# The last layer norm of a hybrid decoder layer: statistics on 128x3 values, spread by identity products, and five tiles scaled on GpSimd

## The chip, the cores and the metric

The kernel runs on one core of a Trainium2 chip. The metric is the device time of one execution in microseconds, the median of several runs. Times inside the execution count from the start of the profiler's span. The engines are TensorE (PE; its weight loads are PEld), VectorE (DVE), ScalarE (ACT), GpSimd (POOL) and SyncE (SP), which issues most of the DMAs.

## What is computed

One inference step of a decoder layer for 256 prompt tokens and 8 x 8 new tokens, 320 tokens together, D = 2048 channels. Two token mixers (an mLSTM and an HGRN2 recurrence) read one input projection; the merged branches go through an output projection, a layer norm, a feed-forward block and a second layer norm. Beside y the new recurrent states are outputs, Cp and Sp (prompt) and Cs and Ss (samples) among them.

```python
x1 = layernorm(alpha * x + merged @ w_out, ln1_g, ln1_b)
hid = square(relu(x1 @ w_up))
y = layernorm(alpha * x1 + hid @ w_down, ln2_g, ln2_b)
# layernorm over the 2048 channels of each token:
mu = mean(x); var = mean(square(x - mu))
(x - mu) * rsqrt(var + 1e-5) * g + b
```

The change concerns the second of these layer norms.

## The kernel before, in words

Activations are held with channels on partitions: 16 tiles of 128 channels x 320 tokens (`self.acc`, one buffer f3m). So the mean and the variance of a token are sums over partitions and over the 16 tiles. Weights stream through in 128x128 blocks. Each fp32 weight and activation is split into a high and a low part in fp32r, and a product is three fp32r matmuls (`mm`, recorded at L341); the statistics use plain fp32 matmuls, which the profile shows as two instructions each. ACT's instructions are recorded at L335, SP's DMAs at L344.

The order of the work on each engine is written by a small scheduler in the kernel (`Sched`). Work is described by generator chains that ask for an engine with an estimated cost, wait for events (`wait`, `post`), and acquire and release buffers (`acq`, `rel`). The scheduler keeps an estimated clock for each engine, and places an instruction when the estimate says that its inputs are ready. Each engine then executes its instructions in exactly that order, waiting where an input is late. The main loop `run_main` lays down the weight matmuls and lets the chains put theirs between them (`pump`). The estimates decide the order alone; the times come from the chip.

In the last weight stage (w_down, f = 3) each finished tile is added on DVE (`ev_dn`, L2138) and enters two running sums over the tiles: S1 of the values and S2 of their squares (`ln_sum`, L1986 and L1987, squares on ACT). A rough mean per token was subtracted before (L2137), so that the sums are well conditioned.

- `ln_pre`: as soon as tile 14 is in, S1 and S2 are multiplied by a 128x128 matrix of ones on TensorE, 320 tokens wide. That sums over the partitions and leaves each sum on all 128 partitions of a PSUM bank. These two products lie between the last weight matmuls.
- `ln_final`: tile 15 (z) and its square are added to the same banks by two further ones products. Then, on values of 128x320: the mean and its square on ACT; variance (L2020) and eps (L2023) on DVE; Ln and Exp on ACT; one Newton step of three DVE instructions (L2027 to L2029). The event "end" says that 1/sigma is ready.
- `y`: DVE subtracts the mean and multiplies by 1/sigma in steps of two tiles, 128x640 (L2154). `yb_`: ACT multiplies by g and adds b, tile by tile; SP issues the y DMA of two tiles.

Meanwhile TensorE makes the prompt states: `m_C`, 8 products of six fp32r matmuls of 512 columns (Cp), each copied from PSUM by ACT and sent out, and `h_S`, 8 products of 256 columns (Sp), copied in four pairs by ACT or DVE. The DMAs of y, Cp and Sp all stand in SP's queue, in the scheduler's order. POOL's queue holds memsets and, late, the six loads for `m_C` (L1193, L1194), the last of them at 2228 us.

Of the kernel before, what the change touches and what calls it, by code (L numbers as in the profile page):

```python
# [246 lines left out]
def post(ev):  # L247
    return ("set", ev)
# [48 lines left out]
class Program:  # L297
# [883 lines left out]
    def m_C(self, h):  # L1181

        late = h >= 2
        if late:

            yield wait(self.rest_ev)
            x = self.wr.rearrange("p u n -> p (u n)")[:, 1536 * (h - 2):1536 * (h - 1)]
            xk, xv = x[:, 0:512].rearrange("p (s k) -> p s k", s=2), x[:, 512:1536]
        else:
            k = yield acq(self.kx)  # L1190
            w = yield acq(self.vx)
            xk, xv = k[:, 1].bitcast(F32), w[:, 1024:2048].bitcast(F32)
        yield ("pool", 1000, lambda: self.nc.gpsimd.dma_start(xk, self.kD[h].rearrange("(s p) k -> p s k", p=128)))  # L1193
        t = yield ("pool", 1000, lambda: self.nc.gpsimd.dma_start(  # L1194
            xv.rearrange("p (n k) -> p n k", k=128), self.vtD[h].rearrange("j (i p) k -> p (j i) k", p=128)))
        e = Ev()
        e.t = t + 5000.0
        yield wait(e)
        if late:
            k = yield acq(self.kx)  # L1200
            w = yield acq(self.vx)
        yield from self.split(xk, k[:, 0], k[:, 1], 512)
        yield from self.split(xv, w[:, 0:1024], w[:, 1024:2048], 1024)
        yield wait(self.main_end)
        for c in range(2):
            if h or c:
                yield wait(self.ln[1]["fin"])
            b = yield acq(self.mbank)
            yield ("pe", 6 * pe_r(512), lambda: [self.mm(
                b.rearrange("p (j v) -> p j v", j=4), k[:, x, s, 128 * c:128 * c + 128], self.of_tokens(w[:, 1024 * y:1024 * y + 1024], s), start=n == 0, stop=n == 5)  # L1210
                for n, (s, x, y) in enumerate((s, x, y) for s in range(2) for x, y in ((0, 0), (0, 1), (1, 0)))])
# [728 lines left out]
    def ln_add(self, n, j, z, pre):  # L1940
# [49 lines left out]
    def ln_pre(self, n):  # L1990

        p = self.ln[n]["p"] = yield acq(self.sbank, 2)
        for i in range(2):
            yield ("pe", pe_f(TOK), lambda: self.mm(p[i][:, :TOK], self.ones, self.lnb[i], start=True, stop=False))
        yield post(self.ln[n]["pre"])

    def ln_final(self, n, z):

        v = self.nc.vector
        st = self.ln[n]  # L2000
        M, RS, X, T = (self.lnb[i] for i in (3, 4, 5, 6))
        q = yield acq(self.tmp)
        t = yield ("act", act(TOK), lambda: self.A(q, z, AF.Square))
        if n:
            yield wait(st["pre"])
        else:
            S1, S2 = self.lnb[0], self.lnb[1]
            yield ("dve", dve(TOK), lambda: v.tensor_tensor(S1, S1, z, ALU.add), (t - act(TOK) - LAT,))
            yield ("dve", dve(TOK), lambda: v.tensor_tensor(q, S2, q, ALU.add), (t,))
            st["p"] = yield acq(self.sbank, 2)  # L2010
            yield wait(self.slack(1000.0))
        p1, p2 = (p[:, :TOK] for p in st["p"])
        yield ("pe", pe_f(TOK), lambda: self.mm(p1, self.ones, z if n else S1, start=n == 0, stop=True))
        yield ("pe", pe_f(TOK), lambda: self.mm(p2, self.ones, q, start=n == 0, stop=True))
        yield rel(self.tmp, q)
        yield post(st["fin"])
        t = yield ("act", act(TOK, True), lambda: self.A(M, p1, scale=1.0 / D))
        st["m"].t = t
        yield ("act", act(TOK, True), lambda: self.A(T, p1, AF.Square, scale=1.0 / D))
        yield ("dve", dve(TOK, True), lambda: v.scalar_tensor_tensor(X, p2, 1.0 / D, T, ALU.mult, ALU.subtract))  # L2020
        for p in st["p"]:
            yield rel(self.sbank, p)
        yield ("dve", dve(TOK, mode=2), lambda: v.tensor_scalar(T, X, 0.0, EPS, ALU.max, ALU.add))  # L2023
        yield post(st["x"])
        yield ("act", act(TOK), lambda: self.A(RS, T, AF.Ln))
        yield ("act", act(TOK), lambda: self.A(RS, RS, AF.Exp, scale=-0.5))
        yield ("dve", dve(TOK), lambda: v.scalar_tensor_tensor(X, T, -0.5, RS, ALU.mult, ALU.mult))  # L2027
        yield ("dve", dve(TOK), lambda: v.tensor_tensor(X, X, RS, ALU.mult))  # L2028
        yield ("dve", dve(TOK), lambda: v.scalar_tensor_tensor(RS, X, 1.5, RS, ALU.add, ALU.mult))  # L2029
        yield post(st["end"])  # L2030
        if n == 0:

            yield ("dve", dve(TOK), lambda: v.tensor_tensor(T, T, RS, ALU.mult))

    def ln_x(self):

# [110 lines left out]
    def y(self):  # L2147
# [1 line left out]
        v = self.nc.vector  # L2149
        st = self.ln[1]  # L2150

        def step(i, n, by, op):
            z = self.acc[:, i:i + n, :]
            return ("dve", dve(n * TOK), lambda: v.tensor_tensor(z, z, by.unsqueeze(1).to_broadcast([128, n, TOK]), op), (0.0,))  # L2154

        sub = lambda i, n=2: step(i, n, self.lnb[3], ALU.subtract)
        yield wait(st["m"])
        yield sub(0, 1)
        yield wait(st["x"])
        yield sub(1, 1)  # L2160
        yield sub(2)
        yield wait(st["end"])
        for i, n in (*((2 * i, 2) for i in range(7)), (14, 1), (15, 1)):
            t = yield step(i, n, self.lnb[4], ALU.mult)
            for j in range(i, i + n):
                self.s.spawn(self.yb_(j, self.acc[:, j, :]), 0, t)
            if i < 12:
                yield sub(i + 4)

    def yb_(self, j, z):  # L2170
        g, b = self.vec[:, V_G2 + j:V_G2 + j + 1], self.vec[:, V_B2 + j:V_B2 + j + 1]
        yield ("act", act(TOK, False, 2), lambda: self.A(z, z, AF.Identity, scale=g, bias=b))
        if j % 2 or j == 14:
            q = slice(j if j > 13 else j - 1, j + 1)
            yield ("sp", 620, lambda: self.dma(self.d["y"][:, q, :], self.acc[:, q, :]))


    def run(self, pool):
# [18 lines left out]
        self.ln = [dict(c=Ev(), x=Ev(), end=Ev(), pre=Ev(), m=Ev(), fin=Ev(), s=[Ev() for _ in range(KT)]) for _ in range(2)]  # L2197
# [85 lines left out]
```

## Time and profile before

| | |
|---|---|
| median of 3 runs | 2266.55 us (2266.45 to 2266.98) |
| profiled execution, time | 2266.39 us |
| profiled execution, span | 2264.5 us |
| TensorE busy | 2256.1 us, granted clock 0.999 |
| DVE busy | 1422.4 us |
| ACT busy | 1014.1 us |
| POOL busy | 13.4 us |
| last add of a w_down tile | 2239.09 us |
| last DMA issued, end of issue | 2259.81 us |

The profile is of one execution; its rows give start, duration, engine, line and the tiles written and read, with the number of instructions that a row merges. A duration of a matmul contains its way through the array, so that matmuls that follow each other overlap in the rows; the distance of their starts is what they take. "[1.44 <-PE ...]" is idle time ahead of an instruction, and what ended it.

### The profile page before, as it was taken

Reading aid. Unit: us, or ns where it says so; the run is one execution under the profiler, and the core shown is the slowest. Engines: PE = TensorE matmul, PEld = TensorE weight load, DVE = VectorE, ACT = ScalarE, POOL = GpSimd, SP = SyncE. Lnnn points to the kernel's source line nnn. Section 1 sums busy time; section 2 is a strip of 40 time slices with the busy share of each in tenths; the row PEclk is TensorE's granted clock in tenths of the full one; section 3 lists DMA queues with packets and bytes.
Section 4 is the critical chain, followed back from the end, with each engine's and each line's share of the span. In section 5 each row is a group of like instructions: output and inputs, shape, how many; then the busy total and the mean of one; then the engine's idle time right before and its main releaser. Section 6 shows DMA issues by size and latency. Waiting matters only on the chain.

```text
span 2264.5 us, 39898 instructions
## 1 busy us (share of the span) xinstructions
PE 2256.1 (100%) x15938; PEld 2217.7 (98%) x15938; DVE 1422.4 (63%) x2490; ACT 1014.1 (45%) x1586; POOL 13.4 (1%) x41
## 2 busy tenths in 40 slices
PE   9999999999999999999999999999999999999998
PEld 9999999999999999999999999999999999999998
DVE  6757667788888876555555769444444444444566
ACT  5444444455555565444434446333433343334434
POOL 0000000000000000000000000000000000000000
PEclk9999999999999999999999999999999999999999
DMA  7888797677677765555556544444444444444644
GB/s 240 305 270 287 224 289 245 200 232 235 197 228 217 235 193 173 173 173 173 174 175 208 193 147 153 151 151 151 149 149 149 149 149 151 150 151 152 198 149 159
DMA packets 251171, 432.94 MB, mean 191 GB/s; under 512 B 106844, under 2 KB 146916, under 8 KB 250984
## 3 DMA queue, kind: packets, MB, share of 16 engines
q1 hardware_dynamic: 250088, 427.24, 58.3%
q0 software_dynamic: 896, 3.15, 0.5%
q8 instruction: 125, 2.05, 0.4%
q14 instruction: 62, 0.51, 0.1%
HBM read 377.30 MB, written 53.00 MB: 190 GB/s over the span
## 4 chain that ended last, share of the span: by engine, by line
PE 99%; ACT 1%; DVE 0%; issue 0%; ACTq 0%; POOL 0%; POOLq 0%
PE bank L341 99%; ACT f3m L335 0%; ACT oC L335 0%; PE bank L1346 0%; PE bank L1118 0%; PE bank L1042 0%; ACT f2l L335 0%; ACT oS L335 0%; DVE f3m L2154 0%; PE bank L1678 0%; ACTq L2279 0%; DVE f2l L2029 0%; DVE f2l L2027 0%; DVE f2l L2028 0%; DVE f2l L2020 0%
## 5 line engine op out<-in xcount | busy, mean ns | idle before, releaser
L341 PE MATMUL bank<-xh,wh 128*128 128x320 f32 x2408 | 751.9, 313 | 0.0
L341 PE MATMUL bank<-xh,wl 128*128 128x320 f32 x2408 | 743.1, 310 | 0.0
L341 PE MATMUL bank<-xl,wh 128*128 128x320 f32 x2408 | 740.2, 308 | 0.0
L335 ACT ACTIVATE wh<-wr 128x1024 fp32r<-128x1024 f32 (+1 forms) x432 | 452.9, 1048 | 582.2 <-PE bank L341 551.8
L511 DVE TENSOR_TENSOR wl<-wr,wh 128x1024 fp32r<-128x1024 f32 x423 | 516.7, 1222 | 304.1 <-ACT wh L335 298.3
L341 PEld LDWEIGHTS bank<-xh,wh 128*128 128x128 f32 x2408 | 452.0, 188 | 6.9 <-issue 3.9
L341 PEld LDWEIGHTS bank<-xl,wh 128*128 128x128 f32 x2408 | 452.3, 188 | 2.7
L341 PEld LDWEIGHTS bank<-xh,wl 128*128 128x128 f32 x2408 | 453.0, 188 | 0.0
L335 ACT ACTIVATE bb<-wr 128x1024 fp32r<-128x1024 f32 x181 | 191.8, 1060 | 352.6 <-PE bank L341 339.9
L511 DVE TENSOR_TENSOR bb<-wr,bb 128x1024 fp32r<-128x1024 f32 x179 | 219.1, 1224 | 159.7 <-ACT bb L335 159.6
L341 PE MATMUL bank<-xh,bb 128*128 128x320 f32 (+1 forms) x1280 | 284.1, 309 | 0.0
L341 PE MATMUL bank<-ra,bb 128*128 128x320 f32 x1264 | 283.3, 308 | 0.0
L341 PE MATMUL bank<-rxb,bb 128*128 128x320 f32 x1112 | 255.0, 309 | 0.0
L341 PE MATMUL bank<-ra,wh 128*128 128x320 f32 x892 | 248.8, 308 | 0.0
L341 PEld LDWEIGHTS bank<-xh,bb 128*128 128x128 f32 x1280 | 214.6, 188 | 0.0
L341 PEld LDWEIGHTS bank<-ra,bb 128*128 128x128 f32 x1264 | 210.6, 188 | 0.2
L341 PE MATMUL bank<-xl,bb 128*128 128x320 f32 (+1 forms) x640 | 197.5, 309 | 0.0
L341 PEld LDWEIGHTS bank<-rxb,bb 128*128 128x128 f32 x1112 | 188.3, 188 | 0.2
L341 PE MATMUL bank<-rxb,wl 128*128 128x320 f32 x596 | 183.7, 308 | 0.0
L341 PE MATMUL bank<-rxb,wh 128*128 128x320 f32 x596 | 183.7, 308 | 0.0
L341 PEld LDWEIGHTS bank<-ra,wh 128*128 128x128 f32 x892 | 161.4, 188 | 0.0
L341 PEld LDWEIGHTS bank<-xl,bb 128*128 128x128 f32 x640 | 120.2, 188 | 0.0
(332 smaller groups left out, 2103.7 us busy)
## 6 DMA issues: line engine op xcount, KB each, us to landing
wr<-wt SPq DMA_DIRECT2D x602, 512.0 KB
rx<-C SPq DMA_DIRECT2D x34, 256.0 KB
Cs<-rx SPq DMA_DIRECT2D x34, 256.0 KB
f<-C SPq DMA_DIRECT2D x30, 256.0 KB
Cs<-f SPq DMA_DIRECT2D x30, 256.0 KB
f<-xT SPq DMA_DIRECT2D x26, 160.0 KB
f<-S SPq DMA_DIRECT2D x8, 512.0 KB
f3h<-S SPq DMA_DIRECT2D x8, 512.0 KB
```

Source lines behind the costliest of these rows:

```text
L335: return self.nc.scalar.activation(out, in_, func, **kw)
L341: self.nc.tensor.matmul(*a, **kw)
L511: self.V().tensor_tensor(lo, raw, hi.bitcast(F32), ALU.subtract)
```

## The change

- For the second layer norm `ln_pre` goes. `ln_final` adds tile 15 and its square to S1 and S2 on DVE, and `ln_rows` follows.
- `ln_rows`: 24 small products with 32 columns of S1 or S2 as the weights and a single column of ones as the moving operand leave the sums with tokens on partitions: 128 x 3 values for each of the sums (320 tokens in three blocks; the last two overlap). Square, variance, eps, Ln, Exp and Newton step work on 128x3. One ones product of S1 leaves the sum of the values on all partitions in a PSUM bank (`pm`), as before.
- 1/sigma comes back to the wide form by three products with the identity matrix as the moving operand and a column of 1/sigma, broadcast to 128 columns, as the weights (`spread`, into the bank `pr`).
- `y` reads both from PSUM: the subtraction is one scalar_tensor_tensor with the factor -1/D, the multiplication a tensor_tensor. Tile 0 stands alone at the beginning and tile 15 at the end; subtraction and multiplication of a pair follow each other.
- `yb_`: tiles 4, 6, 8, 10 and 12 are scaled by GpSimd in place of ACT; a y DMA waits for both of its tiles. In the built program a library reload stands in POOL's queue ahead of its first tile.
- `m_C`: three of the six matmuls of the second Cp product stand ahead of the spread and three behind it; ACT's Cp copies stand behind the Exp.

```diff
@@ m_C
             if h or c:
-                yield wait(self.ln[1]["fin"])
+                yield wait(self.ln[1]["end" if h else "fin"])
             b = yield acq(self.mbank)
-            yield ("pe", 6 * pe_r(512), lambda: [self.mm(...)
+            jobs = [(s, x, y) for s in range(2) for x, y in ((0, 0), (0, 1), (1, 0))]
+            cuts = (0, 6) if h else (0, 1, 2, 3, 6) if c else range(7)
+            for lo, hi in zip(cuts, cuts[1:]):
+                if h == 0 and c and lo == 3:
+                    yield post(self.ln[1]["c1"])
+                    yield wait(self.ln[1]["end"])
+                yield ("pe", (hi - lo) * pe_r(512), lambda: [self.mm(...)
+                    for n, (s, x, y) in enumerate(jobs) if lo <= n < hi])
+            yield wait(self.ln[1]["exp"])
@@ ln_add
-        if j == 14 and n:
-            self.s.spawn(self.ln_pre(n), 0)
@@ ln_final
+        S1, S2 = self.lnb[0], self.lnb[1]
+        t1 = yield ("dve", dve(TOK), lambda: v.tensor_tensor(S1, S1, z, ALU.add), (t - act(TOK) - LAT,))
+        t2 = yield ("dve", dve(TOK), lambda: v.tensor_tensor(q, S2, q, ALU.add), (t,))
         if n:
-            yield wait(st["pre"])
+            yield from self.ln_rows(st, S1, q, t1, t2)
+            return
@@ new
+    def ln_rows(self, st, S1, S2, t1, t2):
+        v = self.nc.vector
+        blocks = (0, 128, TOK - 128)
+        sm = yield acq(self.sm)
+        T, X, RS = (sm[:, 3 * i:3 * i + 3] for i in range(3))
+        p, pm, pr = yield acq(self.sbank, 3)
+        st["pm"], st["pr"] = pm[:, 0:TOK], pr[:, 0:TOK]
+        t = yield ("pe", 700.0, lambda: [self.mm(
+            p[32 * g:32 * g + 32, o:o + 1], S[:, b + 32 * g:b + 32 * g + 32], self.one, start=True, stop=True, skip_group_check=True)
+            for o, (S, b) in enumerate((S, b) for S in (S1, S2) for b in blocks) for g in range(4)], (t1, t2))
+        st["m"].t = (yield ("pe", pe_f(TOK), lambda: self.mm(st["pm"], self.ones, S1, start=True, stop=True))) + 2 * LAT
+        yield post(st["fin"])
+        yield ("act", 200.0, lambda: self.A(T, p[:, 0:3], AF.Square, scale=1.0 / D), (t + 2 * LAT,))
+        yield ("dve", 200.0, lambda: v.scalar_tensor_tensor(X, p[:, 3:6], 1.0 / D, T, ALU.mult, ALU.subtract))
+        yield ("dve", 200.0, lambda: v.tensor_scalar(T, X, 0.0, EPS, ALU.max, ALU.add))
+        yield post(st["x"])
+        yield ("act", 200.0, lambda: self.A(RS, T, AF.Ln))
+        yield ("act", 200.0, lambda: self.A(RS, RS, AF.Exp, scale=-0.5))
+        yield post(st["exp"])
+        t = yield ("dve", 600.0, lambda: (
+            v.scalar_tensor_tensor(X, T, -0.5, RS, ALU.mult, ALU.mult), v.tensor_tensor(X, X, RS, ALU.mult),
+            v.scalar_tensor_tensor(RS, X, 1.5, RS, ALU.add, ALU.mult)))
+        yield post(st["n"])
+        def spread():
+            for i, b in enumerate(blocks):
+                o = max(b, 128 * i)
+                n = min(128, TOK - o)
+                self.mm(pr[:, o:o + n], RS[:, i:i + 1].to_broadcast([128, 128]), self.ident[:, o - b:o - b + n], start=True, stop=True)
+        yield wait(st["c1"])
+        st["end"].t = (yield ("pe", 3 * 218.0, spread, (t,))) + 2 * LAT
@@ y
-        sub = lambda i, n=2: step(i, n, self.lnb[3], ALU.subtract)
+        def sub(i, n=2):
+            z = self.acc[:, i:i + n, :]
+            return ("dve", dve(n * TOK, True), lambda: v.scalar_tensor_tensor(z, wide(st["pm"], n), -1.0 / D, z, ALU.mult, ALU.add), (0.0,))
+        def mult(i, n=2):
+            z = self.acc[:, i:i + n, :]
+            return ("dve", dve(n * TOK, True), lambda: v.tensor_tensor(z, z, wide(st["pr"], n), ALU.mult), (0.0,))
...
+        yield wait(st["x"], st["m"])
         yield sub(0, 1)
-        yield wait(st["x"])
-        yield sub(1, 1)
-        yield sub(2)
+        yield wait(st["n"])
+        yield sub(1)
         yield wait(st["end"])
-        for i, n in (*((2 * i, 2) for i in range(7)), (14, 1), (15, 1)):
-            t = yield step(i, n, self.lnb[4], ALU.mult)
+        for i, n in ((0, 1), *((2 * i + 1, 2) for i in range(7)), (15, 1)):
+            if i > 1:
+                yield sub(i, n)
+            t = yield mult(i, n)
...
-            if i < 12:
-                yield sub(i + 4)
@@ yb_
-        yield ("act", act(TOK, False, 2), lambda: self.A(z, z, AF.Identity, scale=g, bias=b))
-        if j % 2 or j == 14:
-            q = slice(j if j > 13 else j - 1, j + 1)
+        if j in (4, 6, 8, 10, 12):
+            yield ("pool", 700.0, lambda: self.nc.gpsimd.tensor_scalar(z, z, g, b, ALU.mult, ALU.add))
+        else:
+            yield ("act", act(TOK, False, 2), lambda: self.A(z, z, AF.Identity, scale=g, bias=b))
+        yield post(self.y_ev[j])
+        if j % 2 == 0 or j == 15:
+            q = slice(j if j in (0, 15) else j - 1, j + 1)
+            yield wait(*self.y_ev[q])
```

More of the change, by code (lines that the diff above doesn't have):

```diff
@@ L1988, in ln_sum @@
         yield rel(self.tmp, q)
[L1990 to L1995, printed above, removed]
     def ln_final(self, n, z):
@@ L2195, in run @@
         self.vtD = [self.dr.tile([4, 256, 128], F32, name=f"vtD{j}") for j in range(MH)]
-        self.ln = [dict(c=Ev(), x=Ev(), end=Ev(), pre=Ev(), m=Ev(), fin=Ev(), s=[Ev() for _ in range(KT)]) for _ in range(2)]
+        self.ln = [dict(c=Ev(), x=Ev(), end=Ev(), m=Ev(), n=Ev(), exp=Ev(), c1=Ev(), fin=Ev(), s=[Ev() for _ in range(KT)]) for _ in range(2)]
         self.xq, self.xq_ev = [None] * KT, [Ev() for _ in range(KT)]
```

36 lines of the change are left out of this document (13 added, 23 removed).

## The prediction

> **What bounds the kernel now.** I read the page's busy shares and chain first: does anything but TensorE set the end?
>
> ```profile
> PE 2256.1 (100%) x15938; PEld 2217.7 (98%) x15938; DVE 1422.4 (63%) x2490; ACT 1014.1 (45%) x1586; POOL 13.4 (1%) x41
> ...
> PE 99%; ACT 1%; DVE 0%; issue 0%; ACTq 0%; POOL 0%; POOLq 0%
> ```
>
> TensorE owns everything up to the last layer norm. The instruction listings of the two kernels differ only from the last weight stage on, so the timeline from 2233 us is what counts.
>
> ```profile
> 2233.41 0.70 PE L341 MATMUL bank<-f2l,ones 128*128 128x320 f32 x2
> ...
> 2234.83 0.70 PE L341 MATMUL bank<-f2l,ones 128*128 128x320 f32 x2
> ...
> 2238.89 1.55 PE L341 MATMUL bank<-bb,wh 128*128 128x512 f32 x6
> 2239.09 0.49 DVE L2138 TENSOR_TENSOR f3m<-f3m,bank 128x320 f32<-128x320 f32 x1 [1.44 <-PE bank L341]
> ...
> 2240.28 0.70 PE L341 MATMUL bank<-f3m,ones 128*128 128x320 f32 x2
> ...
> 2240.82 0.70 PE L341 MATMUL bank<-f,ones 128*128 128x320 f32 x2
> ...
> 2244.12 0.49 DVE L2027 SCALAR_TENSOR_TENSOR f2l<-f2l 128x320 f32<-128x320 f32 x1 [0.24 <-ACT f2l L335]
> ...
> 2244.65 0.49 DVE L2028 TENSOR_TENSOR f2l<-f2l 128x320 f32<-128x320 f32 x1
> ...
> 2245.70 10.46 DVE L2154 TENSOR_TENSOR f3m<-f3m,f2l 128x640 f32<-128x640 f32 x15
> ```
>
> The last tile's add (L2138) ends at 2239.58, and the first multiplication by 1/sigma starts at 2245.70: 6.1 us of statistics. All that time TensorE is not idle; it works through the Cp products. Then comes the end:
>
> ```profile
> 2254.52 1.02 PE L341 MATMUL bank<-f 128*128 128x256 f32 x4
> ...
> 2256.08 1.03 PE L341 MATMUL bank<-f 128*128 128x256 f32 x4
> ...
> 2258.27 0.40 SPq L344 DMA_DIRECT2D y<-f3m  x1
> 2258.76 1.05 SPq L344 DMA_DIRECT2D Sp<-oS  x2
> ```
>
> and the DMA beside it, in windows (busy times of PE, PEld, DVE, ACT, POOL; granted clock; DMA share; GB/s), and SP's own waits:
>
> ```profile
> 2246.00:2248.00 2.00, 2.00 (x11) 1.65 (x10) 2.00 (x4) 1.66 (x4) 0.00 (x0) 1.00 0.60 227
> ...
> 2254.00:2256.00 2.00, 2.00 (x16) 1.89 (x15) 2.00 (x4) 2.00 (x5) 0.00 (x0) 1.00 1.02 388
> ...
> 2258.00:2260.00 2.00, 0.00 (x0) 0.00 (x0) 0.00 (x0) 0.35 (x1) 0.00 (x0) 1.00 1.03 377
> ...
> 2261.00:2262.00 1.00, 0.00 (x0) 0.00 (x0) 0.00 (x0) 0.00 (x0) 0.00 (x0) 0.50 0.51 201
> ```
>
> ```profile
> SPq L2279 <- DMA Sp<-oS: 2.8, 1, 2.8
> ```
>
> So in the last stage three things finish close together: TensorE (2257.1), SP's last issue (the second of the pair that ends at 2259.81, so at about 2259.4), and the DMA engines, full at some 385 GB/s from 2254 until about 2261.4 (half of the window from 2261) with the outputs y, Cp and Sp. After the data come 3.1 us of closing (2264.5 - 2261.4), which stay. The 6.1 us of statistics matter because nothing of y can leave before them: the DMA has room at 2246 (0.60) and none at 2258. **The output DMA, started late, sets the end; TensorE is the next bound:** its last product could go out from 2257.9 on, a DVE copy later, 1.5 us before it does.
>
> **The change part by part.** All times are on the old kernel's clock.
>
> (1) The two early ones products (2233.41 and 2234.83) go. Two instructions of such a product cost 2 x 0.27 = 0.54 (2240.28 to 2240.82 for the same pair), so the weight stage ends 1.07 earlier and the last add ends at 2238.51. DVE had 1.44 idle ahead of that add, more than 1.07, so it follows.
>
> (2) New ahead of the statistics: S1+z and S2+q on DVE, 0.49 each, the second behind ACT's square: S2 is ready at 2239.55.
>
> (3) The 24 matmuls with a 32-column weight and a one-column moving operand have a twin early in the kernel:
>
> ```profile
> 79.81 0.31 PE L341 MATMUL bank<-misc,f 128*32 128x1 f32 x16
> ```
>
> ```profile
> L341 PEld LDWEIGHTS bank<-misc,f x96: 106/109/113, 79.8 to 379.9; 128*32 128x32 f32 x96
> L341 PE MATMUL bank<-misc,f x96: 170/170/192, 79.8 to 379.9; 128*32 128x1 f32 x96
> ```
>
> Sixteen instructions (eight such products) begin within 0.31 - 0.17 = 0.14, about 10 ns apart. So each half (24 instructions) takes 0.23; if weight loads went one behind the other it would be 24 x 0.106 = 2.5. I take 0.23, the same form in the same rotation over four column groups. S1's half hides in the wait for S2; S2's half runs from about 2239.7 to 2239.95.
>
> (4) The chain on 128x3 values:
>
> ```profile
> L335 ACT ACTIVATE misc<-bank 128x2 f32<-128x2 f32 x13 | 2.2, 166 | 6.3 <-PE bank L341 6.2
> L335 ACT ACTIVATE misc<-misc 128x1 f32<-128x1 f32 x72 | 14.3, 198 | 20.5 <-DVE misc L1148 19.7
> ...
> L1152 DVE TENSOR_TENSOR misc<-misc 128x1 f32<-128x1 f32 x36 | 5.5, 153 | 0.4
> ```
>
> Drain of the matmul 0.17, one ACT square 0.17, two DVE steps of 0.16, Ln and Exp 0.20 each, three DVE steps of 0.16, and 0.03 at each of eight handovers (the rows at 2244.12 and 2244.65 show 0.04 between dependent instructions): 0.17 + 0.17 + 5 x 0.16 + 0.40 + 0.24 = 1.78, to 2241.7. Before, these steps had 320 columns (0.49 each at L2027 and L2028), and ACT put Cp copies between them; the new order on ACT has none inside the chain.
>
> (5) The spread: three fp32 products with up to 128 moving columns. A 320-column pass takes 0.27, so a 128-column one 0.11; six passes 0.64; with weight loads in between perhaps twice that, so 0.5 to 1.3, and I take 0.64. It begins with a weight load behind the wait:
>
> ```profile
> L341 PEld LDWEIGHTS bank<-ra,bb 128*128 128x128 f32 x1264 | 210.6, 188 | 0.2
> ```
>
> With 0.25 for wait and load, and 0.2 for drain and handover, the first multiplication starts at 2241.7 + 0.25 + 0.64 + 0.2 = **2242.8, 2.9 earlier**. The subtractions of tiles 0 to 2 fit into DVE's gaps ahead of it; without that cover they would cost 1.1.
>
> (6) TensorE pays. Removed: four ones products, 2.15. Added: 0.76 for the tiny products with the wait for S2 (from the end of the first Cp group, 2238.89 + 1.37 - 1.07 = 2239.19, to 2239.95), 0.54 for the mean, 0.64 for the spread, and 0.77 idle ahead of it, since the three Cp matmuls put there (1.55 less 0.17 for six, so 0.23 each) end at 2241.2. Sum +0.56: TensorE has no slack in this stage, so its end moves from 2257.1 to 2257.7.
>
> (7) DVE's y loop now subtracts and multiplies the same tile in turn, from PSUM. PSUM costs nothing:
>
> ```profile
> L2138 DVE TENSOR_TENSOR f3m<-f3m,bank 128x320 f32<-128x320 f32 x64 | 31.2, 488 | 87.4 <-PE bank L341 87.2
> L2137 DVE TENSOR_TENSOR f3m<-f3m,f2l 128x320 f32<-128x320 f32 x12 | 5.8, 485 | 0.0
> ...
> L2154 DVE TENSOR_TENSOR f3m<-f3m,f2l 128x640 f32<-128x640 f32 x14 | 10.5, 818 | 0.0
> ```
>
> ```profile
> 2242.66 1.22 DVE L2154 TENSOR_TENSOR f3m<-f3m,f2l 128x320 f32<-128x320 f32 x2
> ```
>
> This last row is one 320-wide and one 640-wide step with nothing between them in need of each other: 1.22 - 0.82 = 0.40 from start to start. Dependent ones stand 0.53 apart (2244.12 to 2244.65). So a 640-wide step takes 0.74 behind an independent one ((10.46 - 2 x 0.40)/13) and about 0.87 behind its own input; a pair of tiles 1.61. From 2242.8: 0.40 + 0.74 + 6 x 1.61 + 1.0 = 11.8, to 2254.6, where it was 2256.16.
>
> (8) GpSimd scales five tiles. ACT loses 5 x 0.57:
>
> ```profile
> 2255.57 2.29 ACT L335 ACTIVATE f3m<-f3m,vec 128x320 f32<-128x320 f32 x4
> ```
>
> which shortens nothing by itself, since ACT then waits for DVE. GpSimd's price isn't in the trace; the nearest rows:
>
> ```profile
> L1467 POOL MEMSET f<- 128x320 f32 x6 | 2.2, 367 | 602.7 <-DVE f L1465 602.7
> ...
> L696 POOL COPY f<-f 128x128 f32<-128x128 f32 x1 | 0.4, 382 | 12.6 <-DMA f<-wif 12.6
> ```
>
> At least the memset's 0.37; the copy scaled to 320 columns is 0.95, and 1.9 if the second operation doubles it. I take 0.8, near the copy. DVE brings a pair every 1.61, so GpSimd keeps up. The first tile counts: y(3,4) is issued at 2242.8 + 2.8 (multiplied) + 0.8 = 2246.4.
>
> (9) The sum goes by the DMA. First data follow an issue by 0.85 (slices of 0.1 us from 2241 on):
>
> ```profile
> 2241.10 0.34 SPq L344 DMA_DIRECT2D Cp<-oC  x1
> ```
>
> ```profile
> DMA  0000000003999989500000000000000000009989
> ```
>
> ```profile
> y<-f3m SPq DMA_DIRECT2D x7, 320.0 KB
> Cp<-oC SPq DMA_DIRECT2D x8, 256.0 KB
> ```
>
> From y(3,4) on, 6 pairs of y (0.328 MB), one single tile (0.164), 7 Cp and 4 Sp (0.262) are left: 5.01 MB at 0.385 MB/us = 13.0, queued without a gap: 2246.4 + 0.85 + 13.0 = 2260.3. The other bound, TensorE 2257.7, DVE's copy 0.69, the issue at 2258.4, 0.85 and 0.68 of data, gives 2260.0. Before: 2261.4. **The end moves by -1.1.** The profiled execution took 2266.39 for a span of 2264.5, 0.16 below the median of 2266.55; so 2265.3 on its clock, 2265.4 against the median.
>
> SP's queue: behind y(3,4), which now waits for GpSimd, stand all later Cp and y; a late GpSimd holds everything. POOL's own queue holds, ahead of its first tile, an instruction that reloads its library, with no wait, behind the last DMA issue there:
>
> ```profile
> 2227.18 1.77 POOL L1194 DMA_DIRECT2D wr<-vtD  x2
> ```
>
> It may start at 2228.95, and the first tile is due at 2245.6: 16.6 us of cover. This trace shows no reload, so its price is open; below 16.6 it is nothing. The Trainium skill (GPSIMD Engine Reference, Instruction dispatch) gives about 6 us for the first call into freshly loaded code; by that estimate the cover is ample and the sum stays.
>
> **The rivals.**
>
> A. *TensorE sets the end and gives the gain back.* It is saturated up to 2257.1, and the spread makes it wait. With the spread at 1.3 and 0.3 more of waking, (6) becomes +1.5; the last issue comes at 2259.4, as before: **2266.4**.
>
> B. *Slower: the tiny products cost their loads.* 48 x 0.106 = 5.1 in place of 0.46 puts TensorE 4.6 later, the last issue at 2263.0, 3.6 past the old: **2270**. It decides from about 31 ns an instruction (1.5 us in all), where (6) has eaten the 1.0 of SP. Against it: the 10 ns of the twin row.
>
> C. *GpSimd at 1.9 a tile* exceeds DVE's 1.61: y(11,12) leaves at 2245.6 + 9.5 = 2255.1 with 2.39 MB from there on (6.2 us): data end 2262.1, **2267.1**. It decides from 1.75.
>
> D. *GpSimd and DVE hinder each other.* The old trace has no stretch where both work wide tiles. If DVE stood still for GpSimd's 4 us, it would end at 2258.6, the last y would leave at 2259.3 with four Sp behind it, 1.21 MB in all: data end 2263.3, 1.9 late, **2268.3**. The Trainium skill (GPSIMD Engine Reference, Specifications) says that the two share their SBUF interfaces and collide where a DVE instruction has two SBUF inputs. Here the new steps have one input in PSUM, so by that rule D doesn't come; it would have with the old L2154.
>
> E. *The reload outlasts its cover*, at 25 us for example: y(3,4) at 2254.8, then 5.01 MB: 2268.7, **2273.6**. It costs from 16.6 on, loses against the old kernel from 17.7 and by over 4.5 from 22.2.
>
> F. *Better:* handovers and GpSimd cheaper by 0.8 together: **2264.6**.
>
> **How the numbers follow.** Forecast 0.61 (2264.9 to 2265.9), A 0.13, B 0.05, C 0.06, D 0.04, E 0.05, F 0.06. The range 2264.5 to 2267.1 holds the forecast, A, C and F (0.86); C stays in as it is the bound of GpSimd's unknown price. A measurement of this kernel tells about 0.2% from no change, 4.5 us: below 2262.0 or above 2271.1. No case gets below (the 13 us of output DMA forbid it), so 0.01; above is E alone, 0.05; the same 0.94.
>
> **What would show it.** The early ones products gone and the last add about 1.1 earlier; 48 matmuls of one column within about 0.7; the first 1/sigma product some 3 us earlier than 2245.7; a TensorE gap of about 0.8 ahead of the spread; GpSimd rows of 0.4 to 1.0; DMA share near 1.0 from 2248 on; the last Sp issue about 1 us earlier. Wrong if the DMA shows gaps after 2249, if y(3,4) waits for GpSimd by more than a microsecond, or if TensorE's last product comes after 2258.7.

## The result and the profile after

| | before | after |
|---|---|---|
| median | 2266.72 us (2265.52 to 2268.06, 22 runs) | 2263.77 us (2263.04 to 2265.14, 22 runs) |
| ratio after / before | | 0.9987, 95% interval 0.9981 to 0.9993 |
| profiled execution, time | 2266.39 us | 2263.73 us |
| profiled execution, span | 2264.5 us | 2262.0 us |

The changed kernel is 0.13% faster, 2263.77 us, within the bound of 0.2% that the prediction called no change. But it lies 0.7 us below the range, whose lower end was 2264.5. So the place to look is a difference of 2.5 us between two spans, of which 1.1 was forecast. (The medians lie 2.95 us apart, the two profiled executions 2.66; the account below is of these two executions.)

The first part of the page of after shows 48 more matmuls and the same busy time on TensorE, and GpSimd (POOL) with 3.3 us more than before:

```profile
PE 2256.2 (100%) x15986; PEld 2218.2 (98%) x15986; DVE 1422.1 (63%) x2492; ACT 1010.9 (45%) x1580; POOL 16.7 (1%) x46
```

The timeline of after, from the last tile's add to the first multiplication by 1/sigma (start, duration, engine, line, operation, tiles written and read):

```profile
2237.96 0.49 DVE L2167 TENSOR_TENSOR f3m<-f3m,bank 128x320 f32<-128x320 f32 x1 [1.20 <-PE bank L341]
...
2238.99 0.49 DVE L2004 TENSOR_TENSOR f<-f2l,f 128x320 f32<-128x320 f32 x1
2239.24 0.37 PE L341 MATMUL bank<-misc,f2l 128*32 128x1 f32 x24
2239.53 0.37 PE L341 MATMUL bank<-misc,f 128*32 128x1 f32 x24
2239.83 0.81 PE L341 MATMUL bank<-f2l,ones 128*128 128x320 f32 x2
2239.98 0.17 ACT L335 ACTIVATE misc<-bank 128x3 f32<-128x3 f32 x1 [1.02 <-PE bank L341]
...
2241.47 0.17 DVE L2051 SCALAR_TENSOR_TENSOR misc<-misc 128x3 f32<-128x3 f32 x1
...
2241.69 0.88 PE L341 MATMUL bank<-cst,misc 128*128 128x128 f32 x6 [0.35 <-DVE misc L2051]
2242.38 0.95 PE L341 MATMUL bank<-bb,wh 128*128 128x512 f32 x3
2242.60 1.22 DVE L2189 TENSOR_TENSOR f3m<-f3m,bank 128x320 f32<-128x320 f32 x2 [0.24 <-PE bank L341]
```

The statistics take 4.15 us from the end of the last add (2238.45) to the first multiplication (2242.60), where they took 6.1. With the add itself 1.13 earlier, y starts 3.1 earlier than at 2245.70. The 48 tiny products are the two rows of 24 that begin at 2239.24 and 2239.53; the row after them begins 0.30 behind the second.

The end of the timeline of after:

```profile
2253.80 0.49 DVE L2189 TENSOR_TENSOR f3m<-f3m,bank 128x320 f32<-128x320 f32 x1
...
2256.13 2.55 SPq L344 DMA_DIRECT2D Sp<-oS  x4
2256.49 1.03 PE L341 MATMUL bank<-f 128*128 128x256 f32 x4
...
2257.62 0.69 DVE L1797 COPY oS<-bank 128x512 f32<-128x512 f32 x1 [1.74 <-PE bank L341]
```

DVE's y loop ends at 2254.29 (before 2256.16), TensorE at 2257.52 (before 2257.1), and SP's last issue at 2258.68 (before 2259.81). The windows of after, with the DMA share and GB/s as the last two columns, show the full stretch: 0.87 from 2246 on, full from 2248 to 2260.

```profile
2246.00:2248.00 2.00, 2.00 (x11) 1.65 (x10) 1.93 (x4) 2.00 (x5) 0.80 (x2) 1.00 0.87 332
2248.00:2250.00 2.00, 2.00 (x11) 1.65 (x10) 1.97 (x3) 1.32 (x3) 0.61 (x1) 1.00 1.01 386
...
2258.00:2260.00 2.00, 0.00 (x0) 0.00 (x0) 0.32 (x1) 0.00 (x0) 0.00 (x0) 1.00 1.01 382
```

Up to here the forecast holds within 0.4 us in each of these times. Now the part that it took for constant. First the DMA strip of before from 2259 to 2264.5 (40 slices of 0.14 us, tenths of busy DMA engines, and GB/s below):

```profile
DMA  8997999998997999973000000000000000000002
GB/s 309 454 421 317 391 328 354 384 406 343 402 441 311 421 361 372 447 313 134 15 30 30 15 30 0 0 0 0 0 0 0 0 0 0 0 0 0 0 0 60
```

and the strip of after from 2257 to 2262.5 (same width):

```profile
DMA  9999999989989899998999910000000000000000
GB/s 382 344 380 339 447 387 357 417 298 462 387 343 432 328 417 357 372 432 328 417 372 357 358 30 0 0 0 0 0 0 0 0 0 0 0 0 0 0 0 0
```

In before the full stream stops, and then 15 to 30 GB/s go on for five slices: by the packets' records one DMA engine of the 16 still has its last packets to send, one behind the other, from 2261.68 to 2262.33. In after all engines stop within 0.2 us, the last at 2260.28. Second, GpSimd's part in the closing, from the listing of the closing line (durations in ns, min/median/max); before, then after:

```profile
L2279 POOLq DRAIN  x3: 40/233/7052, 2227.3 to 2264.2; - x3
```

```profile
L2318 POOLq DRAIN  x3: 40/93/1418, 2251.8 to 2261.7; - x3
```

The middle one of the three drains takes 233 ns in before and 93 in after, and the single records show 0.42 us of standstill ahead of the one in before (2263.35 to 2263.77) against 0.09 in after (2261.30 to 2261.39). From GpSimd's first closing semaphore to its last it is 1.13 us in before (2263.27 to 2264.40) and 0.64 in after (2261.23 to 2261.87).

The difference of the spans is then made of three parts with the same sign: the full stream ends 1.40 earlier, one lagging DMA engine is gone (0.65), and GpSimd closes 0.48 faster: 2.53 in all.

### The profile page after: what moved, and what is told of

The parts are those of the page before. It is cut to its first block, busy times and chain, and to the rows that moved or that the text cites. A ratio compares the mean times of both kernels' runs of the same rounds, so it can differ in the third digit from the quotient of the medians.

```text
span 2262.0 us, 40000 instructions
## 1 busy us (share of the span) xinstructions
PE 2256.2 (100%) x15986; PEld 2218.2 (98%) x15986; DVE 1422.1 (63%) x2492; ACT 1010.9 (45%) x1580; POOL 16.7 (1%) x46
## 4 chain that ended last, share of the span: by engine, by line
PE 100%; DVE 0%; ACT 0%; issue 0%; POOL 0%; DVEq 0%; POOLq 0%
PE bank L341 99%; PE bank L1353 0%; PE bank L1042 0%; PE bank L1118 0%; PE bank L1685 0%; DVE oS L1797 0%; ACT misc L335 0%; PE bank L875 0%; DVE misc L2050 0%; POOL ones L677 0%; DVE misc L2044 0%; DVE misc L2051 0%; DVE misc L2043 0%; DVEq L1797 0%; POOLq L2311 0%
```

## The experiments

My theory, T1, was these three parts, with two causes that have nothing to do with the layer norm's arithmetic: the lag comes from a 16 KB instruction fetch (a DMA packet of the kind "instruction" in the profile) that takes one DMA engine out of the full stretch, and GpSimd's closing from what its queue held before. The rival, T2: the earlier stream explains all, and the closing is scatter between runs.

Executions differ by some 2 us before the stage in question. So each profile is compared from a common mark: the start of the add of tile 14, the DVE row with 4.01 us idle ahead of it in every one of these kernels (before 2230.97, after 2230.92):

```profile
2230.97 0.49 DVE L2138 TENSOR_TENSOR f3m<-f3m,bank 128x320 f32<-128x320 f32 x1 [4.01 <-PE bank L341]
```

```profile
2230.92 0.49 DVE L2167 TENSOR_TENSOR f3m<-f3m,bank 128x320 f32<-128x320 f32 x1 [4.01 <-PE bank L341]
```

| kernel | mark | end of the full stream after the mark | lagging engine | from the data's end to the span's | mark to the end |
|---|---|---|---|---|---|
| before | 2230.97 | 30.71 | 0.65 | 2.16 | 33.52 |
| after | 2230.92 | 29.36 | 0 | 1.68 | 31.04 |
| e1_all_on_act | 2230.38 | 29.79 | 0 | 2.15 | 31.94 |
| e2_before_gpsimd_touch | 2230.79 | 30.76 | 0.73 | 2.07 | 33.56 |
| e3_before_fetch_moved | 2232.74 | 30.66 | 0 | 2.17 | 32.83 |
| e4_after_fetch_moved | 2233.09 | 29.74 | 0.89 | 1.68 | 32.31 |
| e5_before_gpsimd_count | 2230.54 | 30.66 | 0.64 | 1.71 | 33.01 |
| e6_after_late_start | 2230.72 | 31.02 | 0.65 | 1.75 | 33.41 |
| e7_after_less_cp | 2230.66 | 29.21 | 0 | 1.48 | 30.69 |
| e8_after_early_cp | 2231.54 | 29.43 | 0 | 2.03 | 31.46 |
| e9_before_gpsimd_tiles | 2230.64 | 32.80 | 0 | 1.69 | 34.49 |
| e10_before_gpsimd_psum | 2231.89 | 31.45 | 0.32 | 1.66 | 33.43 |
| e11_after_late_reload | 2231.22 | 29.37 | 0 | 1.71 | 31.08 |

(The ends of the stream are from the records of the single DMA packets of each profiled execution; one execution each. Where one engine lags, the end of the full stream can be read up to 0.07 us earlier, and the lag that much longer.)

### e1_all_on_act: the statistics alone

```diff
-        if j in (4, 6, 8, 10, 12):
+        if j in ():
```

> The changed kernel with all 16 tiles of y scaled by ACT; GpSimd has no work at the end and no library reload. Theory (three parts: the output data end 1.3 us earlier, one DMA engine no longer lags 0.7 us behind the others because a 16 KB instruction fetch of TensorE has moved out of the full DMA stretch, and GpSimd's drain in the closing is 0.5 us shorter because it worked shortly before): the drain is long again (0.23 us, begun some 0.4 us after the barrier), ACT is nearly full again, time 0.5 to 0.9 us above the changed kernel, about 2264.5. Rival (the earlier output stream explains all, the closing is scatter between executions): at most 0.3 us above, about 2264.0.

Measured: 2264.72 us (2264.02 to 2265.47), ratio to before 0.9991 (0.9982 to 1.0000). Seen from the mark the stream ends 0.43 later than in after, and the closing is back at 2.15. So the statistics with their PSUM operands carry most of the gain, and GpSimd's five tiles are worth about 0.9, half of it in the closing:

```profile
L2318 POOLq DRAIN  x3: 40/238/7521, 2226.7 to 2262.1; - x3
```

### e2_before_gpsimd_touch and e5_before_gpsimd_count: what removes GpSimd's stall

One copy on GpSimd after tile 12 (e2), or nine (e5), in before:

```diff
+        if j == 12:
+            self.s.spawn(self.touch(z), 0)
...
+    def touch(self, z):
+        yield ("pool", 300.0, lambda: self.nc.gpsimd.tensor_copy(self.misc[:, 20:28], z[:, 0:8]))
```

> The old kernel with one more instruction: GpSimd copies 128x8 values behind the scaling of tile 12, nobody waits for the copy. Theory: GpSimd's drain in the closing falls from 0.23 to about 0.09 us and begins at once, 0.5 us in all; 2266.2 where the old kernel has 2266.7. Rival: no change.

Measured: 2266.74 us, ratio 1.0001 (0.9992 to 1.0009), and a closing of 2.07. That GpSimd stalls because it has been idle for long falls with this run: it had worked 7 us before (at 2256.13) and stalled all the same. But the stall of 0.42 stood one instruction earlier (2263.22 to 2263.64, between the two semaphores ahead of the drain). That led to the next run, where nine copies of 128x1 stand in the place of one.

> Before, with nine GpSimd copies of 128x1 behind the scaling of tile 12: no tensor_scalar, no reload, but more instructions in GpSimd's queue. If GpSimd's stall of 0.4 in the closing comes from where its closing instructions lie in its stream (one copy moved the stall by one instruction): the stall leaves the closing or falls before it, tail 0.4 shorter, about 2266.2. Rival (only the reload or the wide work ahead removes it): stall stays, 2266.7.

Measured: 2266.48 us, ratio 0.9999 (0.9990 to 1.0008); the closing is 1.71, 0.45 shorter than in before, and the middle drain is 102 ns:

```profile
L2284 POOLq DRAIN  x3: 40/102/1893, 2255.9 to 2263.3; - x3
```

So neither the wide work nor the reload is needed: a few instructions more in GpSimd's queue take the stall out of the closing. The total shows no difference that can be told (0.1 us), since the medians of before itself lie between 2266.57 and 2266.72 here. The records of GpSimd's queue, counted from the start of the kernel, say more: in before, e1, e2 and e3 the stall stands ahead of the same, the 69th, record. In after a gap of nearly the same size, 0.38 us, stands early, between two of GpSimd's semaphores (2227.31 to 2227.69), where nothing waits for it; e4 and e6 to e10 have it there too, and in e5 and e11 none is seen. That it is the same stall is likely and not shown. What the stall is, is not shown either. A fetch of the queue's own instructions would depend on the place in this way, but no instruction packet appears among before's DMA packets between 2262.34 and 2264.47, around the stall.

### e3_before_fetch_moved and e4_after_fetch_moved: the lagging engine

The windows of 2 us in which TensorE's 16 KB fetch falls (queue, packets, MB, share), in before from 2251 to 2253 and in after from 2243 to 2245:

```profile
q1 hardware_dynamic: 362, 0.72, 96.1%
q8 instruction: 1, 0.02, 2.9%
```

```profile
q1 hardware_dynamic: 104, 0.12, 18.0%
q8 instruction: 1, 0.02, 3.0%
```

One packet of 16 KB keeps one engine for 0.92 us (0.88 to 1.22 over the runs); in before the output data keep the engines nearly full then (96.1%), in after they do not (18.0%). e3 moves the fetch of before forward, e4 that of after backward, by other instructions in TensorE's warm-up at the start of the kernel (e4: 6 wide and 48 tiny products):

```diff
-        for _ in range(9):
+        for _ in range(7):
             ...
+        for i in range(21):
+            g = 32 * (i % 4)
+            self.mm(self.gbank[g:g + 32, 0:1], self.ones[:, 0:32], self.ones[:, 0:1], start=True, stop=True, skip_group_check=True)
```

> The old kernel with two of nine warm-up products at the start replaced by 21 tiny ones, so that TensorE's instruction stream is 76 instructions longer ahead of the end and its last 16 KB fetch comes at about 2243.5 instead of 2251.7 us, while the DMA engines have room. Theory: the data end without the lagging engine, 0.7 us earlier; 2266.0. Rival: no change.

> The changed kernel with three of nine warm-up products replaced by 48 tiny ones, 180 instructions more, so that a 16 KB fetch of TensorE's instructions falls at about 2251.5 us, in the full DMA stretch. Theory: one DMA engine lags, the data end 0.7 us later; 2264.5. Rival: no change, 2263.8.

Measured: e3 2266.42 us, ratio 0.9999 (0.9990 to 1.0007); e4 2266.79 us, ratio 1.0001 (0.9992 to 1.0010). By the totals alone e3 would be a miss and e4 would prove too much. In the profiled executions all that lies ahead of the mark is longer by 1.8 and 2.2 us (marks at 2232.74 and 2233.09). Whether the edit does this is not shown: the profiled execution of e3 is itself 1.0 us above the median of its kernel. Seen from the mark, the theory holds in both directions: e3 has its fetch at 2243.57 and no lag, and its end comes 0.69 earlier than that of before; e4 has it at 2252.99, and lone packets go on for 0.89 behind the full stream. The strip of e4 from 2260 to 2265.4:

```profile
DMA  9989999999999999898810000000000000000000
GB/s 387 413 353 432 323 414 362 377 410 334 425 364 410 379 364 410 349 440 334 319 46 15 30 30 15 30 30 0 0 0 0 0 0 0 0 0 0 0 0 0
```

The tail of 15 to 30 GB/s is the one of before, now in the kernel that had none. GpSimd's closing stays short in e4 (1.68) and long in e3 (2.17): two separate causes. T2 falls with these runs and e5: lag and stall follow the edits and not chance, though each rests on one profiled execution per kernel. The other runs agree for the lag: before, e2, e5 and e4, with the 16 KB fetch in the nearly full stretch, lag by 0.64 to 0.89; e9 and e10, where the DMA has holes during the fetch or just behind it, by 0 and 0.32; after, e1, e3, e7, e8 and e11, with the fetch before the full stretch, by 0. The exception is e6, below. The size of a lag is not worked out: before and e4 have a hole of 0.4 us behind the fetch as well, and lag all the same.

### e6_after_late_start: does the start of y set the end?

```diff
         yield wait(st["end"])
+        q = yield acq(self.tmp)
+        yield ("dve", 0.0, lambda: [v.tensor_tensor(q, self.lnb[2], self.lnb[2], ALU.add) for _ in range(4)], (0.0,))
+        yield rel(self.tmp, q)
```

> After, with four idle DVE additions of 320 columns (about 1.6 us together) between the subtraction of tile 1 and the first multiplication by 1/sigma; the order of everything else is that of after. If the output DMA, by the moment at which y can start, sets the end of the data: y(3,4) is issued 1.6 later and the data end 1.2 to 1.6 later than in after (2261.5 to 2261.9 in place of 2260.3), about 2265.2 in all. Rival (TensorE and what follows its last product set the end, y only keeps the DMA busy): the last Sp is issued at the same time, data end later by 0 to 0.4, about 2263.8 to 2264.2.

Measured: 2266.78 us (2265.72 to 2267.93), ratio to before 1.0000 (0.9991 to 1.0010): all of the gain is gone.

```profile
2243.65 0.49 DVE L2198 TENSOR_TENSOR f<-f2l 128x320 f32<-128x320 f32 x1
2244.06 1.21 DVE L2189 TENSOR_TENSOR f3m<-f3m,bank 128x320 f32<-128x320 f32 x2
```

The first multiplication comes 13.34 after the mark, in after 11.68: 1.66 later. The full stream ends at 31.02 in place of 29.36: 1.66 later. The delay goes through one for one, as the DMA sum has it. TensorE ends at the same place as in after (26.59 after the mark, in after 26.60), so it doesn't set this end, and the rival's 0 to 0.4 falls. The rest of the loss was not expected: a lagging engine of 0.65 is there again, though TensorE's 16 KB fetch is early (2243.25). An 8 KB fetch by another instruction queue falls into the full stretch at 2259.16; it took 0.31 us. The packet records give the rest: behind it, each starting where the one before ends, come three packets of 2048 bytes of 0.13, 0.27 and 0.23 us, where the median is 0.084. With the fetch that is 0.67 us lost on one engine, and the lag is 0.65. Such slow packets, of 0.15 to 0.28 us, stand next to a fetch in every profile that lags and in e9; after, e1, e3, e7, e8 and e11 have none behind 2247. So a fetch of either queue can make the lag, and it costs the engine more than its own time.

### e7_after_less_cp and e8_after_early_cp: the second bound

```diff
+            if h < 2:
                 yield ("sp", 620, lambda: self.dma(self.d["Cp"][h, :, c, :], self.oC[h][:, c, :]))
```

> After without the four Cp transfers of the heads 2 and 3 (that part of Cp isn't written, 1.05 MB less to send; all arithmetic stays). If only the DMA's bytes set the end, the data end 2.7 us earlier (1.05 MB at 0.385 MB/us), about 2261 in all. If TensorE's last product with its copy and issue is a second bound close behind, as the prediction worked out, the data end at 2259.9 to 2260.0, 0.3 to 0.4 earlier, about 2263.4.

Measured: 2263.62 us (2263.11 to 2264.37), ratio to before 0.9984 (0.9975 to 0.9993). 1.05 MB less to send, and the data end 0.41 earlier on the clock, 0.15 seen from the mark. The window of e7 from 2254 to 2256 shows the DMA all but idle while TensorE is full:

```profile
2254.00:2256.00 2.00, 2.00 (x15) 1.89 (x15) 0.71 (x2) 1.84 (x4) 0.00 (x0) 1.00 0.17 64
```

SP's last issue ends 27.76 after the mark in both kernels. So TensorE's last product with its copy, issue and data is a bound 0.15 us behind the DMA, which the prediction had at 0.3 (2260.0 against 2260.3). e8 tried to use that: the second Cp goes out while the DMA has room, and the last two Sp go one by one.

```diff
+            if h == 0 and c:
+                self.c1_bank, self.ln[1]["c1b"].t = b, 0.0
+                return
+            yield from self.m_out(h, c, b)
...
+        if h >= HH - 2:
+            yield ("dve", dve(256, True), lambda: self.nc.vector.tensor_copy(self.oS[:, h:h + 1, :], b[:, o].rearrange("p (a v) -> p a v", a=1)))
+            yield ("sp", 620, lambda: self.dma(self.d["Sp"][:, h:h + 1, :], self.oS[:, h:h + 1, :]))
...
+        if j == 0:
+            yield ("sp", 620, lambda: self.dma(self.d["y"][:, 0:1, :], self.acc[:, 0:1, :]))
+            yield wait(self.ln[1]["c1b"])
+            yield from self.m_out(0, 1, self.c1_bank)
+            return
```

> An attempt at a better version. After, but ACT copies the second Cp product right behind the scaling of tile 0, so that its transfer goes out while the DMA has room (2244 to 2246), and the last two Sp products are copied and sent one by one (256 columns each). By two close bounds: 0.26 MB leaves the full stretch, worth 0.7 by the DMA; the TensorE bound gets 0.2 to 0.3 shorter by the smaller last copy. Data end 0.4 to 0.6 earlier than in after, about 2263.2. Rival: the later start of y(1,2) and y(3,4) behind the copy (0.5) eats it up: 0 to 0.2, about 2263.6 to 2263.8.

Measured: 2264.49 us (2263.88 to 2265.49), ratio to before 0.9991 (0.9982 to 0.9999): no better than after, a miss. y(3,4) did not start later, so the rival's reason falls too; the Cp did leave early. What it made room for came as a hole:

```profile
2254.00:2256.00 2.00, 2.00 (x18) 1.95 (x17) 1.06 (x3) 1.98 (x4) 0.00 (x0) 1.00 0.77 295
```

With the DMA's store of work smaller, it waits for the last y and Sp, whose time TensorE and ACT set; the stream ends 29.43 after the mark, as in after. Its closing is also longer (2.03 in place of 1.68): 0.22 of the difference stands ahead of the last but one of GpSimd's semaphores (2262.55 to 2262.82), and why is open. Apart from e7, which leaves out part of Cp, none of these runs has a lower median than after.

### e9_before_gpsimd_tiles and e10_before_gpsimd_psum: GpSimd beside DVE

e9 is the other half of the change: before, with GpSimd scaling the five tiles.

```diff
-        yield ("act", act(TOK, False, 2), lambda: self.A(z, z, AF.Identity, scale=g, bias=b))
+        if j in (4, 6, 8, 10, 12):
+            yield ("pool", 700.0, lambda: self.nc.gpsimd.tensor_scalar(z, z, g, b, ALU.mult, ALU.add))
+        else:
+            yield ("act", act(TOK, False, 2), lambda: self.A(z, z, AF.Identity, scale=g, bias=b))
+        yield post(self.y_ev[j])
```

> Before, with GpSimd scaling the tiles 4, 6, 8, 10 and 12 in place of ACT, and nothing else of the change. If the gain of after comes from the earlier statistics, this does nothing to the end of the data (ACT waited for DVE): 2261.7 within 0.3; and the GpSimd's stall of 0.4 in the closing tells what made it go in after: if the tensor_scalars with the reload do, the tail is 0.45 shorter, about 2266.3; if not, 2266.7. Rival (GpSimd and DVE hinder each other where a DVE step has both inputs in SBUF, as the old multiplications have): DVE's multiplications next to the five tiles grow from 0.74 by up to 0.6 each, the last y goes out up to 2 us later, up to 2268.5.

Measured: 2267.81 us (2267.10 to 2269.19), ratio 1.0005 (0.9996 to 1.0014), which doesn't tell it from before; seen from the mark it is 0.97 longer than before, though GpSimd's stall in the closing is gone (1.69). The listing of GpSimd's tiles in e9 (ns, min/median/max), and a window with the DMA share:

```profile
L2174 POOL TENSOR_SCALAR f3m<-f3m,vec x5: 606/2146/2460, 2249.3 to 2257.1; 128x320 f32<-128x320 f32 x5
```

```profile
2250.00:2252.00 2.00, 2.00 (x16) 1.88 (x15) 2.00 (x3) 1.72 (x4) 2.00 (x2) 1.00 0.45 165
```

A tile takes up to 2.46 us as long as DVE's multiplications run, and 0.61 once they are done. In after, the same instruction takes 0.61 each time:

```profile
L2207 POOL TENSOR_SCALAR f3m<-f3m,vec x5: 607/610/615, 2245.6 to 2251.9; 128x320 f32<-128x320 f32 x5
```

The y of a pair waits for GpSimd, SP's queue waits behind it, and the DMA is less than half busy from 2250 to 2252. Here the price is on GpSimd: DVE's fifteen multiplications took 11.22 us in place of 10.46, three of them 0.25 longer each. e10 takes away what differs from after, the place of the operands, and keeps order and instruction counts:

```diff
+        if n:
+            M, st["pm"], st["pr"] = p1, p1, p2
...
-        yield ("dve", dve(TOK), lambda: v.scalar_tensor_tensor(RS, X, 1.5, RS, ALU.add, ALU.mult))
+        yield ("dve", dve(TOK), lambda: v.scalar_tensor_tensor(p2 if n else RS, X, 1.5, RS, ALU.add, ALU.mult))
...
-        sub = lambda i, n=2: step(i, n, self.lnb[3], ALU.subtract)
+        sub = lambda i, n=2: step(i, n, st["pm"], ALU.subtract)
-            t = yield step(i, n, self.lnb[4], ALU.mult)
+            t = yield step(i, n, st["pr"], ALU.mult)
```

> The run before this one (before, with five tiles scaled by GpSimd) had GpSimd tiles of 2.1 to 2.5 us beside DVE steps of two SBUF inputs, where after has 0.61. Here the same kernel with the mean and 1/sigma left in two PSUM banks (ACT writes the mean back in place, DVE's last Newton step writes into the other bank), so that each wide DVE step has one PSUM input; instruction counts and order are those of that run. If the shared use of SBUF by GpSimd and DVE makes the tiles slow: five tiles of 0.6, DVE's pair again 0.74 a step (0.76 of delay gone), y(4,5) leaves about 1.7 earlier, data end back to 2261.7 within 0.4, about 2266.3 in all. Rival (the tiles were slow for their place in the old order, the steps, the reload or the clock): still 2 us a tile, 2267.8.

Measured: 2266.97 us (2265.80 to 2268.50), ratio 0.9999 (0.9991 to 1.0008), and the tiles of e10:

```profile
L2176 POOL TENSOR_SCALAR f3m<-f3m,vec x5: 610/612/617, 2251.1 to 2256.9; 128x320 f32<-128x320 f32 x5
```

With one input of DVE's steps in PSUM the tiles take 0.61, in the old order and with the old statistics. The disputed cost is settled: it is the two SBUF inputs. The sum of the expectation was off by 0.7, since the stream ends 31.45 after the mark: the mean written in place put a wait of 0.5 ahead of the variance, and the first multiplication came 0.59 later than in before.

The Trainium skill (SBUF — State Buffer, SBUF: two separate sides) says that the ports which DVE and GpSimd share are a lock and not a shared bandwidth: with two SBUF inputs of a DVE instruction, the one that starts first holds it and the other is blocked. e9 and e10 agree with the condition; that in e9 DVE loses 0.25 in three places and GpSimd about 1.7 on each of three tiles shows who mostly lost here.

### e11_after_late_reload: the cover of the reload

```diff
+        yield ("pool", 100.0, lambda: self.nc.gpsimd.tensor_copy(self.misc[:, 20:23], RS))
         yield post(st["n"])
```

> After, with one GpSimd copy of 128x3 ahead of the library reload in its queue, which waits for 1/sigma (about 2241.7): so the reload's cover in front of GpSimd's first tile (due at 2245.6) shrinks from 16.7 us to 3.8. If the reload costs less than 3.8 us: nothing, 2263.8. If it costs some 6 us: the first tile starts near 2247.8, y(3,4) leaves 2.2 later, and by the late start run (1.6 late gave the end of the data 1.7) the data end about 2 later, 2265.8 to 2266.5. From 10 us on, over 2269.

Measured: 2264.57 us (2263.75 to 2265.90), ratio to before 0.9990 (0.9982 to 0.9999). GpSimd in e11, timeline, and the listing of its line:

```profile
2242.00 0.19 POOL L2053 COPY misc<-misc 128x3 f32<-128x3 f32 x1 [12.79 <-DVE misc L2051]
2245.90 0.61 POOL L2208 TENSOR_SCALAR f3m<-f3m,vec 128x320 f32<-128x320 f32 x1 [3.71 <-DMA y<-f3m]
```

```profile
L2208 POOLq MODIFY_POOL_CONFIG  x2: 7/9/11, 2242.1 to 2242.2; - x2
```

The reload shows as two instructions of 7 and 11 ns behind the copy. The first tile starts 14.68 after the mark, in after 14.67 (2245.59), and the span ends at 31.08 in place of 31.04. So the reload costs less than the 3.7 us that it had; the 0.8 between the medians of e11 and after is not in these stages. The figure of about 6 us that the prediction cited from the Trainium skill (GPSIMD Engine Reference, Instruction dispatch) would have put the tile some 2 us later; no run here shows it.

## Why the prediction was right in its steps and wrong in its number

- (1) The weight stage, tile 14's add to tile 15's: 8.12 before, 7.04 after, 1.08 shorter (forecast 1.07). Right.
- (2) to (4) S2 was ready at 2239.48 (2239.55), the tiny products were done by 2239.83 (2239.95), the chain at 2241.64 (2241.7). Rival B fell: the twin row early in the kernel gave the right price, and the duration of a single weight load did not.
- (5) First multiplication at 2242.60 (2242.8). The spread took 0.69 from its start to the next matmul (0.64); its wait was 0.05 and not 0.25.
- (6) TensorE's end 2257.52 (2257.7). Ahead of the spread it lost 0.76 by the distance of starts (0.77): the three Cp products in front start at 2240.24 and take 3 x 0.23, the spread starts at 2241.69. The row's 0.35 counts from the end of a duration that contains the way through the array. Rival A did not come, but e7 shows how near it was: 0.15 behind the DMA.
- (7) DVE's end 2254.29 (2254.6); PSUM inputs cost nothing (0.82 for a 640-wide step from either).
- (8) GpSimd 0.61 a tile (0.8, bounds 0.37 and 1.9); y(3,4) issued at about 2246.2 (2246.4). Rival C fell by the same row, rival E by e11. Rival D named a true mechanism and the right reason why it doesn't come here; e9 shows, with the old statistics, what GpSimd's tiles cost without the PSUM inputs: 0.97 from the mark, though its closing is shorter, mostly through GpSimd's tiles and SP's queue, and with 0.76 in all through DVE, where D put 4. The new statistics without PSUM inputs were not run.
- (9) The data ended at 2260.28 (2260.3), and e6 shows that the start of y sets it one for one. **The step that failed is the term behind that, taken over from the prediction's first part into the sum of (9): "After the data come 3.1 us of closing (2264.5 - 2261.4), which stay."** They did not stay: from the end of the data to the span's end it is 1.68 in after. Nor were the 3.1 all closing. 2261.4 had been read as half of a window; the full stream of before ended at 2261.68. Behind it came 0.65 of one lagging engine and 0.48 of a GpSimd stall; only 1.68 of the rest stayed (0.28 misread + 0.65 + 0.48 + 1.68 = 3.09). e3, e4 and e6 show the first with its cause, e1, e2 and e5 the second, with a cause that is only narrowed down.

With the three parts the sum is 2266.39 - 2.53 = 2263.86, where the profiled execution took 2263.73. That is an account and no test, since the parts were read from the same two profiles; the test is in the runs. The range failed for the same reason: all of its cases shared the constant closing, and none of them could go below 2264.5.

SP's own waits in after answer to the row of before with 2.8 for the last Sp:

```profile
SPq L2318 <- DMA Sp<-oS: 1.9, 1, 1.9
...
SPq L2318 <- DVEq L2318: 0.5, 1, 0.5
```

The wait of 2.8 held the last 0.65 of the one engine, as part of 0.9 that it fell by. It was there to be read ahead of the run, with the strip of DMA slices up to the very end.

## What to carry to other kernels

Read the last microseconds packet by packet before they are called constant: what ends after the main stream may belong to one DMA engine or one queue, and an edit that only shifts the instruction streams moves it. Ask of work given to GpSimd beside DVE how many inputs of the DVE steps lie in SBUF; here PSUM as the home of the broadcast operand made the difference between 0.61 and 2.46 us a tile. When two bounds are a few tenths of a microsecond apart, relief for one of them is worth no more than that distance, so price both first: e7 gained 0.15 from the mark and e8 nothing.

## What the runs showed of the hardware that was not expected

- A 16 KB instruction fetch holds one DMA engine for 0.92 us, and some output packets beside it take two to three times as long as the others. Where such a fetch fell into the nearly full stretch, the engine didn't catch up, and the end waited 0.64 (e5) to 0.89 us (e4) for it; e6 shows 0.65 for an 8 KB fetch close to the end. With the fetch in a free stretch nothing is seen (after, e3). In e9 a fetch at 2251.26 caused no lag: the DMA had holes then (0.45).
- GpSimd can stall 0.42 us, and where depends on how many instructions its queue held: one more moved the stall by one instruction (e2), nine more took it out of the closing (e5).
- In the profiled executions the mark lies between 2230.38 and 2233.09, more than most of the effects that were looked for. The mark inside the kernel, and not the total, made the runs readable.
